# Reordering the last tiles' tails at the two hand-overs into the up projections of a two-layer decoder trunk

## The chip, the cores and the metric

One Trainium2 chip, one core of it. The metric is device time in microseconds (us) of the whole kernel, as the median of repeated runs; one further execution was profiled, and every duration below is from that one.

## The reference

An inference step of a two-layer trunk on 1024 prompt tokens and 64 sample tokens (8 x 8), width 1024, all in float32. Layer 0 is an S5 state-space mixer with a gated output, layer 1 a differential attention; each is followed by a convolutional feed-forward block. What matters here is the border between a mixer and its feed-forward block:

```python
out = gl[..., :D_MODEL] * jax.nn.sigmoid(gl[..., D_MODEL:])          # layer 0: gl = z @ glu_w
x = x + rmsnorm(a_out, p['a_post_g'][i])                             # layer 1: rmsnorm(o @ w_o, b_post_g)
f_out, buf = conv_ffn(rmsnorm(x, p['f_pre_g'][i]), ...)              # h = x @ w_up; conv over 3 tokens; gelu*val; @ w_down
```

Per token row there are so two norms between the mixer's matmul and the up projection `w_up` (1024 x 5632): one on the mixer's output, and, after the residual is added, one ahead of `w_up`.

## The kernel before

The 1088 tokens are nine row tiles: 0 to 7 are 128 prompt tokens each, the ninth (NTT) holds the 64 sample tokens. A float32 product is made of three matmuls on split operands (L815 to L817, `mm3`), a high part and a low part each; ScalarE (ACT) writes a high part (L150) and VectorE (DVE) the low part (L151).

**The mixer's end.** `glu` (layer 0) and `o_proj` (layer 1) go through the tiles in two batches, EARLY = sample, 0, 3, 1, 4 and LATE = 2, 5, 6, 7. For each finished tile they call `tail.add`, which does the following.

- `tail_a` (L847 to L861): loads the residual row tile into an `xr` slot by DMA (L853; there are two such slots), takes the sum of squares on ACT (L830), multiplies by the gain (L857), takes the reciprocal root (`rstd_from`), adds the residual (L860) and stores the row (L861).
- `tail.norm` for the tile before it: again a sum of squares and a reciprocal root, and the product with the gain (L870).
- `tail.pop`, once more than `lag` tiles are queued: the tile is transposed on TensorE (PE, L876) and split into `xT_hi` and `xT_lo` (`tail_b`). For tiles 3, 4 and 5 `Combos.pair` forms four differences with tile 0, 1 and 2 (L917 to L920), then five groups of four transposes; three of these go to the `Combos` tiles, which the up projection's seven-product scheme reads.

`lag` is 2 in `glu` and 1 in `o_proj`. With `root` off, `rstd_from` starts from an integer trick and makes three Newton steps of two small DVE instructions (L129, L136, L140); with it on, ACT takes a square root (L126), DVE a reciprocal (L127), and one step follows. `root` is off in `glu` and on from `ffn_down` on, so also in `o_proj`.

**The up projection.** `ffn_up` handles 22 inner tiles f. `inputs(f)` loads two 512 KB weight pieces, forms four sums in two `xr` slots (L1117 to L1120: `s12`, then `s34`), splits four operands on ACT and DVE and takes two `acc` slots, hg and hv. `first(f)` makes seven products of 12 matmuls each for the tiles 0 to 5; `rest(f, s)` then makes two products of 24 matmuls over tiles 6, 7 and the samples. For f = 0 the two are interleaved with the tails that are still open:

```python
        inputs(0)
        g = first(0)
        for _ in range(3):
            next(g)
            tail.pop()
```

The three parts of `first(0)` are: two products with tiles 0 to 2 (24 matmuls, with the copy L1154 of the first into hv between them); four products with the pair sums and tiles 3 to 5; one more with pair sums. So ahead of this loop the queue holds tiles 5, 6, 7 after `glu`, and 6, 7 after `o_proj`, all of them normed by a last `tail.norm()`.

**What sets the order.** The tile framework orders the instructions of each engine ahead of time by its own simulated timeline (`schedule_with_timeline_sim=True`): the order of the program gives the priority, readiness in that timeline decides. So the first weights of `inputs(0)` stand among the last tiles of `glu` in the trace. On the chip each engine takes its instructions in the order so fixed, and SP issues all the DMAs named here from one queue. Slots: `acc` has 14 buffers, of which 8 hold the Combos, one each the two gains (`post` and the gain of the second norm) and four the LATE rows; `gr` has 5, `xr` 2, `raw` (weights as loaded) 2. A new tile waits until its slot is given back.

Of the kernel before, what the change touches and what calls it, by code (L numbers as in the profile page):

```python
# [21 lines left out]
D = 1024  # L22
# [51 lines left out]
def trunk_kernel(ctx, tc, I, O):  # L74
# [30 lines left out]
    x1d = dpool.tile([T, D], F32, tag="x1d", name="x1d")  # L105
# [657 lines left out]
    EARLY, LATE = ORDER_O[:5], ORDER_O[5:]  # L763
# [40 lines left out]
    def slot(tag, shape=None, dtype=F32):  # L804

        al = {"gx": "acc", "post": "acc", "junk": "gr"}
        shp, bufs = {"acc": ([P, 2 + SEQ + NB * 10], NACC), "gx": ([P, 4, 2 * P], NACC), "gr": ([P, 512], NGR),
                     "xr": ([P, D], 2), "junk": ([P, D], NGR), "post": ([P, D], NACC),
                     "cvo": ([P, 4, 18], 2), "cpar": ([P, 2 * NF, 20], 1), "ss": ([P, 1], 4)}[tag]
        tag = al.get(tag, tag)  # L810
        return pools["ph"].tile(shape or shp, dtype, tag=tag, name=nm(tag), bufs=bufs)
# [7 lines left out]
    def tokens(tt):  # L819
        return (tt * P, P) if tt < NTT else (SEQ, TS)  # L820

    def row_bcast(src):
        t = slot("post")
        nc.sync.dma_start(t, src.partition_broadcast(P))
        return t

    def square_sum(y, n):
        junk = slot("junk", dtype=BF16)
        ss = slot("ss")
        A.activation(junk[0:n, 0 : y.shape[1]], y, AF.Square, accum_out=ss[0:n])  # L830
        return ss[0:n]
# [15 lines left out]
    def tail_a(y, tt, post, xsrc, xdst, last=False, rest=slice(0, D), aside=False, xr=None):  # L847


        t0, n = tokens(tt)  # L850
        if xr is None:
            xr = slot("xr")
            nc.sync.dma_start(xr[0:n], xsrc(tt))  # L853
        halves = (slice(512, D), slice(0, 512)) if last else (slice(0, D),)
        ss = square_sum(y[:, rest], n)
        for hs in halves if last else (rest,):
            V.tensor_tensor(y[:, hs], y[:, hs], post[0:n, hs], ALU.mult)  # L857
        r = rstd_from(pools["ph"], ss, 1, n, "n1", bufs=4, pre=sums.pop(tt, None), aside=aside, root=tail.root)
        for hs in halves:
            V.scalar_tensor_tensor(y[:, hs], y[:, hs], r[0:n], xr[0:n, hs], op0=ALU.mult, op1=ALU.add)  # L860
            nc.sync.dma_start(xdst(tt)[:, hs], y[:, hs])  # L861
# [17 lines left out]
    def tail_b(y, tt, scale=None):  # L879

        t0, n = tokens(tt)
        for h in range(2):
            split_evac(xh[:, 4 * h : 4 * h + 4, t0 : t0 + n], xl[:, 4 * h : 4 * h + 4, t0 : t0 + n],
                       transposed(y[:, 512 * h : 512 * h + 512], n), scale)
# [6 lines left out]
    class Combos:  # L891
        def __init__(self):
            self.tiles = [slot("acc", [P, 3, HT], F32R) for _ in range(8)]
# [32 lines left out]
    class Tail:  # L926
# [3 lines left out]
        def __init__(self):  # L930
            self.n, self.q, self.combos, self.gain, self.lag = [], [], None, None, 2

            self.root = False

        def add(self, y, tt, *a, aside=False, **kw):
            tail_a(y, tt, *a, aside=aside, **kw)
            self.norm()
            self.n.append((y, tt, aside))
            if len(self.q) > self.lag:
                self.pop()  # L940

        def norm(self):
            for a in self.n:
                tail_n(*a, self.gain)
            self.q += [a[:2] for a in self.n]
            self.n = []
# [10 lines left out]
    tail = Tail()  # L957
# [9 lines left out]
    def x_scr(buf):  # L967
        def f(tt):
            t0, n = tokens(tt)
            return buf[t0 : t0 + n]  # L970
        return f
# [31 lines left out]
    def fold_sample(dst, ps, t=None):  # L1003

        t = slot("gr") if t is None else t
        A.copy(t[0:TS], ps[TS : 2 * TS])
        V.tensor_tensor(dst, ps[0:TS], t[0:TS], ALU.add)
# [15 lines left out]
    def glu(ws):  # L1023

        zt = slot("acc")[0:TS, 0:D]
        zv = zt.rearrange("r (b g c) -> r b g c", g=8, c=16)
        for u in range(3):
            for j in range(min(3, 8 - 3 * u)):
                zs = zsd.rearrange("(b u) r w -> u r b w", u=3)[u, 32 * j : 32 * j + NB]
                nc.sync.dma_start(zv[:, :, 3 * u + j], zs.rearrange("s b (t c) -> (s t) b c", c=16))  # L1030
        post = row_bcast(I["a_post_g"][0])
        tail.gain = row_bcast(I["f_pre_g"][0])
        ao = {}


        for q, tts, end in ((0, ORDER_U, ()), (1, ORDER_U, ()), (2, EARLY, ()), (3, ORDER_O, EARLY), (2, LATE, LATE)):
            if q or end:
                ws = glu_units(q)
            qs_ = slice(q * 256, (q + 1) * 256)
            for tt in tts:  # L1040
                t0, n = tokens(tt)
                if tt in EARLY and q == 0 or tt in LATE and end is LATE:
                    ao[tt] = slot("acc")
                if end is LATE:
                    for cs in (slice(0, 512), slice(768, D)):
                        nc.sync.dma_start(ao[tt][:, cs], aod[t0 : t0 + n, cs])
                if q == 0 and tt == ORDER_U[4]:
                    tail_b(zt, NTT)
                    xsx = sample_pair()
                ps = tok_mm(tt, ws, None if n == P else xsx)  # L1050
                if n < P:
                    g = slot("gr")[0:n]
                    fold_sample(g, ps)
                else:
                    g = ps
                sg = slot("gr")[0:n]
                A.activation(sg[:, 0:256], g[:, 256:512], AF.Sigmoid)
                yq = ao[tt][0:n, qs_] if tt in ao else sg[:, 256:512]
                V.tensor_tensor(yq, g[:, 0:256], sg[:, 0:256], ALU.mult)
                if tt in end:  # L1060
                    if tt == 0:
                        tail.combos = Combos()
                    tail.add(ao[tt][0:n, 0:D], tt, post, x_in, x_scr(x1d), rest=qs_, aside=tt in EARLY)
                else:
                    part(yq, tt, post, qs_)
                    if tt in LATE:
                        nc.sync.dma_start(aod[t0 : t0 + n, qs_], yq)
                        tail.norm()
                        tail.pop()
            if q == 0:  # L1070
                conv_params(0)
                lam_column(cpool)
        tail.norm()


    NPAR = 20
# [20 lines left out]

    def ffn_up(i, down):
        cp = pools["cpar"]
        tail.gain = None  # L1100
        wv = I["w_up"][i].rearrange("(kt p) f -> p kt f", p=P)
        u3 = lambda t: t.rearrange("p (k f) -> p k f", f=P)

# [123 lines left out]

        inputs(0)
        g = first(0)
        for _ in range(3):  # L1230
            next(g)
            tail.pop()
        while tail.q:
            tail.pop()
        for s in range(2):
# [770 lines left out]
    def o_proj():  # L2006

        ws = half_units(I["w_o"][0], 1)
        post = row_bcast(I["b_post_g"][0])
        tail.gain, tail.lag, tail.root = row_bcast(I["f_pre_g"][1]), 1, True  # L2010
        conv_params(1)
        xsx = sample_pair()

        for half, tts in ((1, ORDER_O), (0, LATE)):
            if half == 0:
                ws = half_units(I["w_o"][0], 0)
            hs = slice(512 * half, 512 * half + 512)
            os_ = slice(512 - 512 * half, D - 512 * half)
            for tt in tts:
                if tt == 0 and half:  # L2020
                    tail.combos = Combos()
                t0, n = tokens(tt)
                end = half == 0 or tt in EARLY
                if end:
                    y = slot("acc")[0:n, 0:D]
                    nc.sync.dma_start(y[:, os_], yod[t0 : t0 + n])
                    if half:
                        part(y[:, os_], tt, post, os_)
                    yh = y[:, hs]
                else:  # L2030
                    yh = slot("gr")[0:n]
                ps = tok_mm(tt, ws, xsx)
                if n == P:
                    A.copy(yh, ps)
                else:
                    fold_sample(yh, ps)
                if end:
                    tail.add(y, tt, post, x_scr(x2d), x_scr(x3d), rest=hs, aside=tt in EARLY)
                else:
                    part(yh, tt, post, hs)  # L2040
                    nc.sync.dma_start(yod[t0 : t0 + n], yh)
                    tail.norm()
                    tail.pop()
        tail.norm()

    dtile = lambda name, shape: dpool.tile(shape, F32, tag=name, name=name)
    x2d = dtile("x2d", [T, D])
    gd = dtile("gd", [NF, P, TG])
    aod = dtile("aod", [SEQ, D])
    x3d = dtile("x3d", [T, D])  # L2050
# [62 lines left out]
```

## Time and profile before

| | |
|---|---|
| median of 3 runs | 2666.85 us (2663.87 to 2669.19) |
| the profiled execution | 2665.99 us, its span 2664.1 us |
| PE matmul busy | 2493.7 us, 94% |
| DVE busy | 1947.8 us, 73% |
| ACT busy | 1281.0 us, 48% |
| POOL busy | 661.2 us, 25% |
| chain that ended last | PE 58%, DVE 13%, DMA 4%, issue 4%, ACT 3%, POOL 3% |

Busy time is time in which an engine executes; the chain that ended last is followed back from the last instruction, at each step to what released it. The share of busy time is a mean over stages: the two stretches that the change touches, some 36 us each, are read by themselves. They are called hand-over 1 (after `glu`, 434.8 to 471.4 us) and hand-over 2 (after `o_proj`, 1888.9 to 1924.6 us).

### The profile page before, as it was taken

Reading aid. Unit: us, or ns where it says so; the run is one execution under the profiler, and the core shown is the slowest. Engines: PE = TensorE matmul, PEld = TensorE weight load, DVE = VectorE, ACT = ScalarE, POOL = GpSimd, SP = SyncE. Lnnn points to the kernel's source line nnn. Section 1 sums busy time; section 2 is a strip of 40 time slices with the busy share of each in tenths; the row PEclk is TensorE's granted clock in tenths of the full one; section 3 lists DMA queues with packets and bytes.
Section 4 is the critical chain, followed back from the end, with each engine's and each line's share of the span. In section 5 each row is a group of like instructions: output and inputs, shape, how many; then the busy total and the mean of one; then the engine's idle time right before and its main releaser. Section 6 shows DMA issues by size and latency. Waiting matters only on the chain.

```text
span 2664.1 us, 39516 instructions
## 1 busy us (share of the span) xinstructions
PE 2493.7 (94%) x14234; PEld 2199.5 (83%) x14234; DVE 1947.8 (73%) x3543; ACT 1281.0 (48%) x2597; POOL 661.2 (25%) x1062
## 2 busy tenths in 40 slices
PE   3778998999999999999999899999899999998997
PEld 2777876999999977788777788877799999996776
DVE  7994358677777789984222688875877777778999
ACT  6763234444444454354322677764544444444433
POOL 3220030111111176501201222113011111127571
PEclk9999998999999999999999899999899999999999
DMA  5443233122222233445646333325322222233334
GB/s 144 104 97 88 84 126 126 58 76 78 85 72 78 81 117 97 125 134 183 207 158 210 104 83 96 98 93 173 127 69 79 75 75 74 75 98 105 92 107 154
DMA packets 265688, 286.77 MB, mean 108 GB/s; under 512 B 42268, under 2 KB 212564, under 8 KB 265492
## 3 DMA queue, kind: packets, MB, share of 16 engines
q1 hardware_dynamic: 261892, 273.55, 33.3%
q0 software_dynamic: 3088, 9.77, 1.7%
q8 instruction: 113, 1.85, 0.3%
q10 hardware_dynamic: 512, 0.92, 0.1%
q14 instruction: 83, 0.68, 0.1%
HBM read 193.58 MB, written 70.93 MB: 99 GB/s over the span
## 4 chain that ended last, share of the span: by engine, by line
PE 58%; DVE 13%; DMA 4%; issue 4%; ACT 3%; POOL 3%; SPq 0%; DVEq 0%; ACTq 0%; POOLq 0%
PE mm L815 17%; PE mm L817 17%; PE mm L816 17%; DVE acc L1437 2%; PE mm L1426 2%; DVE xT_lo L151 2%; DMA gr<-gd 2%; DVE S L1907 1%; ACT S L1911 1%; DVE xT_hi L151 1%; DVE wst L151 1%; PE mm L1935 1%; PE tr L876 1%; DVE acc L860 1%; POOL xr L1306 1%
## 5 line engine op out<-in xcount | busy, mean ns | idle before, releaser
L815 PE MATMUL mm<-xT_hi,whi 128*128 128x384 f32 (+1 forms) x1408 | 457.0, 325 | 2.0 <-ACT acc L1154 1.7
L816 PE MATMUL mm<-xT_lo,whi 128*128 128x384 f32 (+1 forms) x1408 | 456.2, 324 | 1.4 <-DVE xT_lo L151 1.4
L817 PE MATMUL mm<-xT_hi,wlo 128*128 128x384 f32 (+1 forms) x1408 | 454.0, 324 | 0.0
L815 PEld LDWEIGHTS mm<-xT_hi,whi 128*128 128x128 f32 x1408 | 265.4, 189 | 3.8 <-ACT acc L1154 2.4
L816 PEld LDWEIGHTS mm<-xT_lo,whi 128*128 128x128 f32 x1408 | 265.7, 189 | 2.2 <-DVE xT_lo L151 2.1
L817 PEld LDWEIGHTS mm<-xT_hi,wlo 128*128 128x128 f32 x1408 | 265.3, 189 | 0.8
L1203 POOL COPY cvo<-acc 128x2 f32<-128x2 f32 x88 | 54.2, 616 | 814.1 <-ACT acc L1186 814.0
L815 PE MATMUL mm<-whi,xT_hi 128*128 128x512 f32 x608 | 242.9, 404 | 5.8 <-ACT whi L798 5.8
L1200 DVE SCALAR_TENSOR_TENSOR acc<-acc,cpar,acc 128x1104 f32<-128x1104 f32 x176 | 239.9, 1385 | 4.7 <-ACT acc L1198 4.7
L816 PE MATMUL mm<-wlo,xT_hi 128*128 128x512 f32 x608 | 242.8, 400 | 0.1
L817 PE MATMUL mm<-whi,xT_lo 128*128 128x512 f32 x608 | 242.2, 400 | 0.0
L150 ACT CAST whi<-raw 128x1024 fp32r<-128x1024 f32 x88 | 92.7, 1053 | 248.5 <-PE mm L817 245.1
L1437 DVE TENSOR_TENSOR acc<-mm,acc 128x512 f32<-128x512 f32 x279 | 184.3, 679 | 8.4 <-PE mm L817 8.1
L151 DVE TENSOR_TENSOR wlo<-raw,whi 128x1024 fp32r<-128x1024 f32 x88 | 107.7, 1224 | 103.5 <-PE mm L816 90.8
L815 PE MATMUL mm<-acc,whi 128*128 128x384 f32 x528 | 178.8, 339 | 2.5 <-DVE acc L1160 2.5
L817 PE MATMUL mm<-acc,wlo 128*128 128x384 f32 x528 | 178.9, 339 | 0.0
L816 PE MATMUL mm<-acc,whi 128*128 128x384 f32 x528 | 178.3, 338 | 0.0
L815 PEld LDWEIGHTS mm<-whi,xT_hi 128*128 128x128 f32 x608 | 115.3, 190 | 36.9 <-ACT whi L798 6.2
L816 PEld LDWEIGHTS mm<-wlo,xT_hi 128*128 128x128 f32 x608 | 115.2, 189 | 27.9 <-DVE wlo L799 0.8
L817 PEld LDWEIGHTS mm<-whi,xT_lo 128*128 128x128 f32 x608 | 114.9, 189 | 27.9 <-issue 0.8
L1198 ACT ACTIVATE acc<-acc,cpar 128x1104 f32<-128x1104 f32 x88 | 114.2, 1313 | 18.1 <-DVE acc L1169 11.9
L1186 ACT COPY acc<-mm 128x256 f32<-128x256 f32 x88 | 32.4, 369 | 183.7 <-PE mm L817 183.7
(575 smaller groups left out, 6311.6 us busy)
## 6 DMA issues: line engine op xcount, KB each, us to landing
raw<-in_w_up_dram SPq DMA_DIRECT2D x88, 512.0 KB
gd<-acc SPq DMA_DIRECT2D x44, 552.0 KB
raw<-in_w_down_dram SPq DMA_DIRECT2D x44, 512.0 KB
gr<-gd SPq DMA_DIRECT2D x80, 256.0 KB
raw<-in_glu_w_dram SPq DMA_DIRECT2D x40, 256.0 KB
acc<-in_cache_k_dram SPq DMA_DIRECT2D x16, 512.0 KB
acc<-in_cache_v_dram SPq DMA_DIRECT2D x16, 512.0 KB
xj<-in_x_prompt_dram SPq DMA_DIRECT2D x8, 512.0 KB
```

What stands on the lines that cost most here:

```text
L150: A.copy(hi_ap, ps_ap)
L151: V.tensor_tensor(lo_ap, ps_ap, hi_ap.bitcast(F32), ALU.subtract)
L815: PE.matmul(out, lh, rh, start=start, stop=False, **kw)
L816: PE.matmul(out, lh, rl, start=False, stop=False, **kw)
L817: PE.matmul(out, ll, rh, start=False, stop=stop, **kw)
L860: V.scalar_tensor_tensor(y[:, hs], y[:, hs], r[0:n], xr[0:n, hs], op0=ALU.mult, op1=ALU.add)
L1186: A.copy(hb[:, 2 + n0 : 2 + SEQ], ps[:, 0:wp])
L1198: A.activation(hc, hb[:, 2 : 2 + TG], AF.Identity, bias=cp[:, ft, 3:4], scale=cp[:, ft, 2:3])
L1200: V.scalar_tensor_tensor(hc, hb[:, tap : tap + TG], cp[:, ft, tap : tap + 1], hc, op0=ALU.mult, op1=ALU.add)
L1203: GP.tensor_copy(co[:, 0:2], hb[:, SEQ : SEQ + 2])
L1426: PE.matmul(pa[h], lt, wt[:, h * 512 : (h + 1) * 512], start=st and j == 0, stop=sp and j == len(seq) - 1)
L1437: V.tensor_tensor(a, ps, a, ALU.add)
```

## The change

- `Tail.last` takes the place of `add` for tile 7, the last of LATE: it pops the tile that is queued (5, a pair) at once and only notes tile 7's arguments.
- `Tail.end` does tile 7's `tail_a`, sets `root` on ahead of it, norms tile 6 and lists tile 7 for its norm. `ffn_up` calls it after the first part of `first(0)`, calls `tail.norm()` for tile 7 after the second, and pops both after the third.
- `lag` is 1 for LATE in `glu` too, and is put back to 2 at `glu`'s end; the last `tail.norm()` of `glu` and `o_proj` is gone.

```diff
+        def last(self, *a, **kw):
+            self.pop()
+            self.late = a, kw
+
+        def end(self):
+            (y, tt, *a), kw = self.late
+            self.root = True
+            tail_a(y, tt, *a, **kw)
+            self.norm()
+            self.n.append((y, tt, False))
...
                 if end is LATE:
+                    tail.lag = 1
...
-                    tail.add(ao[tt][0:n, 0:D], tt, post, x_in, x_scr(x1d), rest=qs_, aside=tt in EARLY)
+                    put = tail.last if tt == LATE[-1] else tail.add
+                    put(ao[tt][0:n, 0:D], tt, post, x_in, x_scr(x1d), rest=qs_, aside=tt in EARLY)
...
-        tail.norm()
+        tail.lag = 2
...
     def ffn_up(i, down):
         cp = pools["cpar"]
-        tail.gain = None
...
-        for _ in range(3):
-            next(g)
-            tail.pop()
+        next(g)
+        tail.end()
+        next(g)
+        tail.norm()
+        next(g)
+        tail.gain = None
         while tail.q:
             tail.pop()
...
-                    tail.add(y, tt, post, x_scr(x2d), x_scr(x3d), rest=hs, aside=tt in EARLY)
+                    put = tail.last if tt == LATE[-1] else tail.add
+                    put(y, tt, post, x_scr(x2d), x_scr(x3d), rest=hs, aside=tt in EARLY)
...
-        tail.norm()
```

## Rows read from the trace of the kernel before

**Rows 1.** Page, busy us (share of the span) and instructions of each engine.

```profile
PE 2493.7 (94%) x14234; PEld 2199.5 (83%) x14234; DVE 1947.8 (73%) x3543; ACT 1281.0 (48%) x2597; POOL 661.2 (25%) x1062
```

**Rows 2.** Windows, hand-over 1: us; busy PE, PEld, DVE, ACT, POOL; PEclk (granted); DMA.

```profile
440.00:445.00 5.00, 0.00 (x0) 0.00 (x0) 4.96 (x21) 1.33 (x3) 0.00 (x0) 0.75 0.23 94
450.00:455.00 5.00, 3.87 (x15) 3.47 (x14) 5.00 (x9) 2.77 (x5) 0.31 (x2) 0.50 0.50 150
...
sum 36.40, PE 24.99 PEld 23.58 DVE 30.07 ACT 15.18 POOL 1.46; mean PE 3.57 PEld 3.37 DVE 4.30 ACT 2.17 POOL 0.21
```

**Rows 3.** The windows of hand-over 2, their sum.

```profile
sum 35.60, PE 25.48 PEld 23.78 DVE 32.45 ACT 18.37 POOL 2.25; mean PE 3.64 PEld 3.40 DVE 4.64 ACT 2.62 POOL 0.32
```

**Rows 4.** Timeline of PE in hand-over 1: start, us, engine, line [idle before <-releaser].

```profile
448.76 1.09 PE L876 MATMUL tr<-ident,gr 128*128 128x128 f32 x4 [9.75 <-DVE gr L917]
...
457.23 0.34 PE L816 MATMUL mm<-xT_lo,whi 128*128 128x384 f32 x1
457.40 0.34 PE L817 MATMUL mm<-xT_hi,wlo 128*128 128x384 f32 x1
...
459.14 0.60 PE L876 MATMUL tr<-ident,gr 128*128 128x128 f32 x4
459.49 0.42 PE L816 MATMUL mm<-acc,whi 128*128 128x384 f32 x1
...
471.38 0.31 PE L816 MATMUL mm<-xT_lo,whi 128*128 128x320 f32 x1
```

**Rows 5.** Timeline of DVE in hand-over 1.

```profile
437.77 1.28 DVE L860 SCALAR_TENSOR_TENSOR acc<-acc,rr,xr 128x1024 f32<-128x1024 f32 x1
438.97 1.28 DVE L870 SCALAR_TENSOR_TENSOR acc<-acc,rr,acc 128x1024 f32<-128x1024 f32 x1
...
440.23 0.68 DVE L1117 TENSOR_TENSOR xr<-raw 128x512 f32<-128x512 f32 x1
...
442.75 1.23 DVE L151 TENSOR_TENSOR wlo<-xr,whi 128x1024 fp32r<-128x1024 f32 x1
...
444.33 1.28 DVE L860 SCALAR_TENSOR_TENSOR acc<-acc,rr,xr 128x1024 f32<-128x1024 f32 x1
...
446.73 0.68 DVE L1119 TENSOR_TENSOR xr<-raw,raw 128x512 f32<-128x512 f32 x1
...
447.93 0.68 DVE L917 TENSOR_TENSOR gr<-acc,acc 128x512 f32<-128x512 f32 x1
...
460.47 1.28 DVE L870 SCALAR_TENSOR_TENSOR acc<-acc,rr,acc 128x1024 f32<-128x1024 f32 x1
```

**Rows 6.** Timeline of POOL and ACT in hand-over 1: hv's slot and the copy into it.

```profile
450.77 0.10 POOL L1129 MEMSET acc<- 128x2 f32 x1 [11.66 <-PE tr L876]
...
452.16 0.47 ACT L1154 COPY acc<-mm 128x384 f32<-128x384 f32 x1
```

**Rows 7.** Waits of PE in hand-over 2: line <- what released it, us, times, longest.

```profile
PE tr L876 <- DVE acc L870: 5.9, 1, 5.9
PE mm L815 <- DVE acc L1160: 2.5, 1, 2.5
PE mm L816 <- DVE xT_lo L151: 1.1, 1, 1.1
```

**Rows 8.** Timelines of DVE and PE in hand-over 2.

```profile
1898.27 0.68 DVE L917 TENSOR_TENSOR gr<-acc,acc 128x512 f32<-128x512 f32 x1
...
1924.60 0.31 PE L815 MATMUL mm<-xT_hi,whi 128*128 128x320 f32 x1
```

**Rows 9.** DVE lines in hand-over 1: xcount, busy us, mean ns, idle before.

```profile
L136 DVE SCALAR_TENSOR_TENSOR rs<-rr,rv 128x1 f32<-128x1 f32 x13 | 2.4, 214 | 0.0
```

**Rows 10.** ACT lines, whole run: loads of the table that holds the square root.

```profile
L126 ACT ACT_TABLE_LOAD x3 | 3.8, 1283 | 0.1
```

**Rows 11.** SP's queue in hand-over 1 (residual of tile 7), and one residual load on the chain.

```profile
430.31 0.42 SPq L853 DMA_DIRECT2D xr<-in_x_prompt_dram  x1
...
1827.37 3.75 DMA xr<-x2d
```

More of the change, by code (lines that the diff above doesn't have):

```diff
@@ L933, in __init__ @@
             self.root = False
+            self.late = None
         def add(self, y, tt, *a, aside=False, **kw):
```

## The prediction

> **What bounds the kernel now.** The page comes first: PE is busy 94% of the span and DVE 73% [rows 1], so a reordering can only win where PE stands still or runs at half its clock. The reader then goes to the two stretches in which the mixer's last tiles run out and the up projection begins. In hand-over 1 PE does nothing for a whole window, then works at a granted clock of 0.50, which is 1.2 of its 2.4 GHz, while DVE is busy 4.96 and 5.00 of 5 us [rows 2].
>
> What is lost there follows from the work. The seven products of `first(0)` are 84 matmuls, 0.173 us apart at full clock (457.23 to 457.40), which is 14.5 us. Tiles 2, 5, 6 and 7 need 44 transposes, four of which take 0.35 us (459.14 to 459.49), so 3.9 us. Together 18.4 us [rows 4]. In hand-over 1 the first matmul of `rest` starts at 471.38, and one product of f = 1 (12 x 0.173 = 2.1 us) has already slipped in ahead of it: of the 36.4 us, 36.4 - 2.1 - 18.4 = 15.9 us are lost. In hand-over 2 `rest` starts at 1924.60 [rows 8]; of the 35.6 us, 17.2 are lost. The pool is 33 us.
>
> The waits then say to whom it goes. In hand-over 1 it is one wait of 9.75 us, for the pair's first difference L917 [rows 4]. Tile 5 was normed by 438.97 + 1.2 = 440.2, but L917 started only at 447.93: DVE first did the first weight sums (L1117), a low part (1.23 us), tile 7's residual sum (444.33), tile 6's norm and the third weight sum (446.73) [rows 5]. hv is another victim: its slot came free with the pair's transposes (450.77), and the copy L1154, behind which the second product waits, ran at 452.16 [rows 6]. In hand-over 2 the longest wait, 5.9 us, is for tile 2's norm (L870), then come 2.5 us for L1160, which stood in DVE's queue, and 1.1 us for a low part [rows 7]. There the pair began at 1898.27 already [rows 8], because `lag` was 1.
>
> **The change, part by part, against the profiled execution of 2665.99 us.** DVE is full in both stretches, so I first bound what any order could give, by DVE's work that must be done ahead of `rest`.
>
> Hand-over 1: DVE's 30.07 us [rows 2] contain the four sums of `inputs(1)` (4 x 0.68 = 2.7, by the duration at 446.73) and one low part of its weights (1.23) [rows 5]; both can wait. With `root` on for three roots, two of three Newton steps fall away in each, 12 small instructions of about 2.4/13 = 0.18 us [rows 9], 2.2 us (L140 taken as its partner L136; the reciprocal replaces L129). With `lag` 1, tile 2's two low parts (2 x 0.68 = 1.4) move in among tile 7's matmuls. What is left is 30.07 - 2.7 - 1.2 - 2.2 - 1.4 = 22.6 us: `rest` at 457.6 at the earliest, against 471.4 - 2.1 = 469.3 now, a gain of 11.7 at most.
>
> Hand-over 2: `root` and `lag` already stand, so only 2.7 + 1.2 come off 32.45 [rows 3]; 1889 + 28.5 = 1917.5 against 1924.6, a gain of 7.1 at most.
>
> **The pair at once.** In hand-over 1 L917 can follow tile 5's norm at 440.2 in place of 447.93, 7.7 us earlier; PE's 9.75 us shrink to about 2, and hv's slot comes as much earlier. One weight sum (0.68) may still come ahead. I take 7.0. The lower end: the residual of tile 7, now behind `s12` in the two `xr` slots, lands late and the whole load stands on the path, 0.42 + 3.75 [rows 11], so -4.2; the upper end is 11.7. In hand-over 2 the pair is early anyway; what can go is the queue before L1160, 2.5 us [rows 7], and I take that; tile 2's wait isn't touched. Lower end: `s12` gets the slot that tile 7's residual had, so two sums and a low part (0.68 + 0.68 + 1.23 = 2.6) can get ahead of tile 2's norm, -2.6; upper end 7.1.
>
> **Tile 7's tail and two norms behind the weights.** Moved are, per hand-over, the residual load of 512 KB (SP; issued at 430.31 now [rows 11]), the sum of squares, the product with the gain, the root, the residual sum, the store of the row, and for tiles 6 and 7 a sum of squares, a root and a product of 1.28 us. Nothing is added to DVE. I cost the move at nothing on PE as long as first(0)'s 14.5 us of products hide it. If the cover is short, `rest` waits: from the end of `s12`'s low part, issue and load (4.2) and the sum and norm (2 x 1.28 with ACT's work between) must pass. On SP the load stands behind the weight loads of `inputs(0)`, long issued, and at worst behind those of `inputs(1)`; queued behind it are the row stores and later weights, for which nobody waits in these 20 us.
>
> **The root on ACT in hand-over 1.** One more table load of 1283 ns [rows 10] and three short activations. ACT is busy 15.18 of 36.4 us [rows 2], so I take 0, with ends 0 and -1.3. The Trainium skill, ScalarE: Activation LUTs, section on table sets, speaks against this: calls should be batched by set, and it prices a switch at about 2.7 us in that section; by that figure on the path the sum would be 2659.2 in place of 2656.5. The trace's load of 1283 ns is half of it, and no row shows one inside a hand-over with PE waiting on it alone.
>
> The `lag` set back and the gain's None moved cost nothing: no instruction.
>
> **Sum.** 7.0 + 2.5 = 9.5 us: 2665.99 - 9.5 = 2656.5 for this execution. It lay 0.9 below the median of 2666.85, so 2657.4 for the median. Ends: a gain of 11.7 + 7.1 = 18.8 (2648.1) and a loss of 4.2 + 2.6 + 1.3 = 8.1 (2675).
>
> **The rivals.**
> *The wait only moves (20%).* The work on DVE stays, and what PE no longer waits for at the pair it waits for at `rest`, on tile 7's norm, which ended at 461.7 while PE had products to run [rows 5]. For it: DVE at 5.00 of 5. Against: PE then has f = 1's first product to take, as now. A gain of 0 to 5: 2662 to 2667.
>
> *The order stays (7%).* The planner places by readiness in its own timeline; where it holds the weight sums ready earlier than tile 5, the trace keeps its order. Against: the pair now has the higher priority. 2666 to 2668.
>
> *Slower: tile 7's residual at the head of DVE's queue (14%).* The load waits for `s12`'s slot; if the planner puts L860 of tile 7 ahead of the low parts of `s34` or the pair, these stand behind a DMA. Price per hand-over: 4.2, one weight load ahead of it in SP's queue (another 3.75 [rows 11]), and PE back at half clock: at 0.50 the 3.87 us of PE in one window [rows 2] lose half, 1.9. That is 9.9, twice 19.7, less the 9.5: 2677 for the median. It decides from a stall of 9.5/2 = 4.8 us in each. Against: the slot is free from `s12`'s low part, which the new order brings forward. The Trainium skill, TensorE: Matmul & The Clock Gate, in its passage on engine queue depths, calls DVE's queue strictly first in, first out; by that this rival has its force, and the trace agrees: L917 stood 7.7 us behind others though its inputs were there.
>
> **How the numbers follow.** 59% for the forecast (2648 to 2661.5), 20, 7 and 14 for the rivals. A measurement can tell 0.2%, 5.3 us, from no change, so faster is below 2661.5: the forecast and a touch of the first rival, 0.60. Same takes the rest of that rival, the second, and nothing else, 0.26; slower 0.14. The range 2648 to 2670 holds the first three cases and leaves out the slower one beyond it.
>
> **What would show it.** Right: L917 of hand-over 1 within 2 us of tile 5's L870, PE's wait there near 2 us, `rest` of f = 0 some 25 us (not 34) after glu's last matmul net of f = 1's product; L1160 in hand-over 2 without a wait. Wrong: a wait of PE for tile 7's low part or transposes of over 4 us, an L860 released by a DMA, L917 still behind L1119, or a first product cut off from its second by hv's slot.

## The result, and the profile after

The changed kernel takes 2671.12 us (median of 20 runs, 2667.82 to 2676.25), the kernel before 2666.03 us (20 runs beside them, 2662.15 to 2669.68). The ratio is 1.0022, with a 95% interval of 1.0016 to 1.0028: slower by 4.3 to 7.5 us, where 9.5 us less had been forecast. The span of the profiled execution is 2668.7 us. The page's first part answers to [rows 1]:

```profile
PE 2493.2 (93%) x14234; PEld 2200.6 (82%) x14234; DVE 1952.4 (73%) x3531; ACT 1279.9 (48%) x2601; POOL 617.6 (23%) x1062
```

The work is the same, and DVE has 12 instructions less, as forecast for the root. From L931 on the lines of the changed kernel are up to 17 higher: L1126 loads a weight piece, L1131 to L1134 form the weight sums, L1168 is the copy into hv.

**Hand-over 1.** The windows that answer to [rows 2]; the third covers the whole stretch, with its sums in it:

```profile
440.00:445.00 5.00, 2.25 (x11) 2.28 (x12) 3.81 (x5) 1.11 (x2) 0.24 (x2) 0.77 0.99 292
450.00:455.00 5.00, 5.00 (x24) 4.96 (x23) 4.87 (x14) 3.50 (x10) 0.00 (x0) 0.71 0.15 61
...
434.80:471.20 36.40, 27.95 (x157) 26.81 (x158) 28.69 (x62) 15.64 (x32) 0.55 (x5) 0.91 0.31 98
```

PE no longer stands for a whole window, and is busy 27.95 us where it was 24.99. Its timeline tells what became of the wait of 9.75 us [rows 4]:

```profile
435.64 0.44 PE L816 MATMUL mm<-xT_lo,whi 128*128 128x384 f32 x1 [0.90 <-DVE xT_lo L151]
442.75 1.09 PE L876 MATMUL tr<-ident,gr 128*128 128x128 f32 x4 [4.92 <-DVE gr L917]
...
448.20 0.66 PE L876 MATMUL tr<-ident,gr 128*128 128x128 f32 x4 [2.65 <-DVE xT_lo L151]
...
467.12 0.31 PE L816 MATMUL mm<-xT_lo,whi 128*128 128x320 f32 x1
```

The wait for the pair is 4.92 us, and two waits for low parts, of 2.65 and 0.90 us, stand beside it. DVE's timeline, which answers to [rows 5], shows why:

```profile
437.06 1.29 DVE L860 SCALAR_TENSOR_TENSOR acc<-acc,rr,xr 128x1024 f32<-128x1024 f32 x1
438.38 0.69 DVE L1133 TENSOR_TENSOR xr<-raw,raw 128x512 f32<-128x512 f32 x1
438.99 0.68 DVE L1134 TENSOR_TENSOR xr<-raw,xr 128x512 f32<-128x512 f32 x1
439.59 1.28 DVE L870 SCALAR_TENSOR_TENSOR acc<-acc,rr,acc 128x1024 f32<-128x1024 f32 x1
440.78 1.23 DVE L151 TENSOR_TENSOR wlo<-xr,whi 128x1024 fp32r<-128x1024 f32 x1
441.93 0.68 DVE L917 TENSOR_TENSOR gr<-acc,acc 128x512 f32<-128x512 f32 x1
...
445.72 1.23 DVE L151 TENSOR_TENSOR wlo<-raw,whi 128x1024 fp32r<-128x1024 f32 x1 [1.90 <-ACT whi L150]
446.86 0.69 DVE L920 TENSOR_TENSOR gr<-acc,gr 128x512 f32<-128x512 f32 x1
447.46 0.68 DVE L151 TENSOR_TENSOR xT_lo<-tr,xT_hi 128x512 fp32r<-128x512 f32 x1
```

The last two weight sums (438.38, 438.99) now go ahead of tile 5's norm, and a low part between that norm and L917, which starts at 441.93. With all four sums made this early the two `raw` buffers come free, and the next inner tile's first weight gets into the middle of the pair: at 445.72 DVE stands 1.90 us for its high part. ACT in turn had waited for that weight's DMA, which SP issued at 439.14:

```profile
444.64 1.05 ACT L150 CAST whi<-raw 128x1024 fp32r<-128x1024 f32 x1 [3.89 <-DMA raw<-in_w_up_dram]
```

L920 and tile 5's low part, which PE wants, stand behind that weight in DVE's order. The Trainium skill, TensorE: Matmul & The Clock Gate, in its passage on engine queue depths, calls DVE's queue strictly first in, first out; the trace agrees, 1.90 us of standing with L920 and the low part behind it.

**Hand-over 2.** The waits of PE from 1880 to 1926 us (line, what released it, us, times, longest), which answer to [rows 7]:

```profile
PE tr L876 <- DVE acc L870: 8.1, 2, 6.7
PE tr L876 <- DVE gr L917: 2.2, 1, 2.2
PE mm L816 <- DVE xT_lo L151: 1.7, 1, 1.7
PE tr L876 <- DVE xT_lo L151: 1.2, 1, 1.2
```

The wait of 2.5 us for L1160 is gone. The 8.1 us for L870 are two waits in PE's timeline:

```profile
1897.13 1.94 PE L876 MATMUL tr<-ident,acc 128*128 128x128 f32 x8 [6.74 <-DVE acc L870]
...
1921.36 0.63 PE L876 MATMUL tr<-ident,acc 128*128 128x128 f32 x4 [1.33 <-DVE acc L870]
```

The first is for tile 2's norm and grew from 5.9 to 6.7 us; the second is for the norm of tile 7, which the change put late and for which PE did not wait before. There are also waits for L917 and for a low part of the pair. DVE started tile 5's norm at 1903.03 and L917 at 1906.53, where it had been 1898.27 [rows 8], behind the last two weight sums (1899.31, 1899.90) and low parts:

```profile
1898.10 1.22 DVE L151 TENSOR_TENSOR wlo<-xr,whi 128x1024 fp32r<-128x1024 f32 x1
...
1901.89 1.22 DVE L151 TENSOR_TENSOR wlo<-xr,whi 128x1024 fp32r<-128x1024 f32 x1
1903.03 1.28 DVE L870 SCALAR_TENSOR_TENSOR acc<-acc,rr,acc 128x1024 f32<-128x1024 f32 x1
1905.39 1.23 DVE L151 TENSOR_TENSOR wlo<-raw,whi 128x1024 fp32r<-128x1024 f32 x1 [1.08 <-ACT whi L150]
1906.53 0.69 DVE L917 TENSOR_TENSOR gr<-acc,acc 128x512 f32<-128x512 f32 x1
```

**Where the time went.** Both kernels run the same 14,234 matmuls and transposes. So the traces can be laid side by side: the start of the matmul with the same number ends a stage, at places where the two orders agree again. A step is the time of a stage less its time in one further execution of the kernel before (span 2665.8 us, the first experiment). In the change three stages move. "Last head" is the end of the attention, 1768 to 1813 us, where its last head runs out into the output projection; the change does not touch it.

| kernel, us | hand-over 1 | up projection, layer 0 | last head | hand-over 2 | ratio (95%) |
|---|---|---|---|---|---|
| before, first profile | -0.9 | 0.0 | 0.0 | 0.0 | 1 |
| the change | -3.4 | 0.0 | **+3.9** | **+2.5** | 1.0022 (1.0016 to 1.0028) |
| hand-over 1 only | -4.0 | 0.0 | +3.7 | 0.0 | 1.0003 (0.9994 to 1.0011) |
| hand-over 2 only | -2.1 | 0.0 | +0.8 | 0.0 | 1.0007 (0.9998 to 1.0016) |
| residual early | -4.4 | +0.1 | -1.1 | -0.3 | 0.9986 (0.9977 to 0.9995) |
| pair at once alone | -1.9 | +4.8 | +1.0 | +0.3 | 1.0048 (1.0035 to 1.0062) |
| residual early, hand-over 1 only | -3.6 | +0.1 | -0.1 | -0.1 | 0.9987 (0.9978 to 0.9996) |
| without root | -0.8 | +4.9 | -1.1 | 0.0 | 1.0032 (1.0021 to 1.0043) |
| lag alone | -0.9 | +7.7 | +3.9 | -0.6 | 1.0057 (1.0044 to 1.0069) |
| change, old order of last head | -5.3 | 0.0 | +0.1 | -0.1 | 1.0000 (0.9991 to 1.0009) |
| hand-over 1, old order of last head | -4.4 | 0.0 | +0.2 | -1.1 | 1.0001 (0.9991 to 1.0010) |
| before, new order of last head | -2.7 | 0.0 | +3.9 | +0.4 | 1.0025 (1.0014 to 1.0036) |

How far one execution can be trusted is seen at hand-over 1: four executions with the old source there gave 0 (the one compared with), -0.9, -2.1 and -2.7, while PE's granted clock over the 38 us from 434 was 0.78 in the first of them and 0.87 in the last. These four mean -1.4, the six with the change there (two of them with the residual early) -4.2. So in the profiled executions hand-over 1 gained 2.8 us; PE's waits say nearly the same: 9.7 + 1.1 + 0.3 + 0.2 = 11.3 us before, 4.9 + 2.7 + 0.9 + 0.2 = 8.7 after. A profiled execution can lie up to 5 us from its kernel's median (4.9 above it with `lag` alone, 5.1 below it with hand-over 1 and the old order), so the ratios are firmer than sums of steps.

### The profile page after: what moved, and what is told of

It reads as the page before. It is cut to its first block, busy times and chain, and to the rows that moved or that the text cites. A ratio compares the mean times of both kernels' runs of the same rounds, so it can differ in the third digit from the quotient of the medians.

```text
span 2668.7 us, 39527 instructions
## 1 busy us (share of the span) xinstructions
PE 2493.2 (93%) x14234; PEld 2200.6 (82%) x14234; DVE 1952.4 (73%) x3531; ACT 1279.9 (48%) x2601; POOL 617.6 (23%) x1062
## 5 line engine op out<-in xcount | busy, mean ns | idle before, releaser
L1217 POOL COPY cvo<-acc 128x2 f32<-128x2 f32 x88 | 48.0, 546 | 839.4 <-ACT acc L1200 839.3
L1924 DVE CUSTOM_DVE_ANT_0 S<-mm,tb 128x512 f32<-128x512 f32 (+3 forms) x192 | 101.4, 552 | 22.9 <-PE mm L1922 19.5
```

The costliest lines, as they stand in the source:

```text
L1217: GP.tensor_copy(co[:, 0:2], hb[:, SEQ : SEQ + 2])
L1924: V.tensor_tensor_reduce(S_[j][:, k0 : k0 + w], ps[:, 0:w], H["tb"][:, b0 : b0 + w], 0.125, -3e38, ALU.add, ALU.max, mx[:, j, c : c + 1])
```

## The experiments

**The kernel before once more**, for the scale of the comparison.

> The kernel before, once more, for the spread of a stage from one execution to the next. If stages are steady: every landmark (start of hand-over 1, of the attention's last head, of hand-over 2) within 1 us of the first profile once the start is aligned; theory C wants 3 us and more between the same landmarks.

Measured 2667.61 us in its one run, the span 2665.8. Against it the first profile differs by +2.4 us at 1236 to 1340 us and by -3.3 us at 1723 to 1745, stages that no kernel here edits; steps are read only where several executions agree.

**One hand-over alone.** `last` and the new loop are used where `tail.late` was set, the old path where it was not. First hand-over 1 only, with these lines of `o_proj` put back:

```diff
-                    put = tail.last if tt == LATE[-1] else tail.add
+                    put = tail.add
...
+        tail.norm()
```

> The change at hand-over 1 alone; o_proj and hand-over 2 as before. Theory A (three places: hand-over 1 gains, hand-over 2 loses, and the shift of the planner's timeline reorders the last head of the attention): hand-over 1 gains 2 to 3 us, the stretch 1765 to 1800 loses 4 to 5, hand-over 2 is as before; together 0 to 4 us slower. Theory B (all of the loss sits in hand-over 2): 2 to 4 us faster. Theory C (what differs between the traces outside the hand-overs is chance of one execution): 2 to 4 us faster too, with the attention's stretch as before.

Ratio 1.0003 (0.9994 to 1.0011). The gain at hand-over 1 is there (-4.0), and 3.7 us are lost again 1300 us later, at the last head, in a stage with the same source text.

Then hand-over 2 only, the same lines of `glu` put back and its `tail.lag = 1` gone:

> The change at hand-over 2 alone; glu and hand-over 1 as before. Theory A: 2 to 4 us slower, all of it in hand-over 2, where the pair's first difference starts some 6 us later than before; the attention's order as before. Theory B: 5 us slower, the whole of the measured loss. If the postponed tail is harmless there: within 1 us.

Ratio 1.0007 (0.9998 to 1.0016); the step at hand-over 2 is 0.0, neither the forecast's gain nor the 2.5 us that the whole change lost there. PE's waits in the same window:

```profile
PE tr L876 <- DVE acc L870: 8.4, 2, 7.4
PE mm L816 <- DVE xT_lo L151: 1.7, 1, 1.7
PE mm L815 <- ACT acc L1167: 1.5, 1, 1.5
```

The wait for L1160 is gone here too. In its place tile 2's norm is waited for longer (7.4 us in place of 5.9), tile 7's norm for 1.1, and the copy into hv (L1167 here) for 1.5, where it was 0.6.

**Tile 7's residual loaded early**, in `last`, so that it holds its `xr` slot while the first inner tile's weights are made, as it did before:

```diff
         def last(self, *a, **kw):
             self.pop()
-            self.late = a, kw
+            t0, n = tokens(a[1])
+            xr = slot("xr")
+            nc.sync.dma_start(xr[0:n], a[3](a[1]))
+            self.late = a, dict(kw, xr=xr)
```

> The change, but tile 7's residual is loaded where it was before, in the call that notes the tile, so that it takes the slot that it had. Slot theory (the postponed load hands its slot to the weight sums of the first inner tile, these free the raw buffers early, and the weights of two inner tiles get ahead of tile 5's norm and of the pair): in hand-over 2 the pair starts again within 2 us of where it was before, in hand-over 1 it follows tile 5's norm; 3 to 7 us faster than before. Rival (the postponed tail itself comes late at the rest product): no better than the change, 3 to 5 us slower than before.

Ratio 0.9986 (0.9977 to 0.9995): one DMA issued earlier makes the change faster than the kernel before. L917 started at 437.75 and 1894.14, and the last head's order was again that of before. By the steps, most of the difference from the change lies in the last head (5.0 us) and hand-over 2 (2.8), and only 1.0 in hand-over 1. Two things changed at once, the slot and the planner's order, so the next runs part them.

**The pair at once, without the move of tile 7's tail** (`lag` 1 in LATE, `root` off):

```diff
         def last(self, *a, **kw):
             self.pop()
-            self.late = a, kw
+            self.add(*a, **kw)
+            self.norm()
```

> The pair at once and lag 1 in glu, but tile 7's tail and both norms straight behind it, ahead of the first inner tile's weights; root as before. Slot theory: tile 7's residual keeps its slot, so hand-over 1 gains as much as with the residual loaded early, 3 to 5 us, and hand-over 2 nothing (within 1 us). The planner's order of the attention's last head differs from before's here too, another order than the change's: if a changed order there costs in itself, plus 1 to 5 us in that stage; if only the change's own order is bad, 0. If postponing the tail is what gains: hand-over 1 within 1 us of before.

Ratio 1.0048 (1.0035 to 1.0062), an outright loss, in neither hand-over: 4.8 us in layer 0's up projection, and 4.6 more in the stage from 1032 to 1235 us. The expected gain of 3 to 5 us at hand-over 1 did not come either: -1.9 lies among the 0 to -2.7 of the old source, although L917 started at 436.52 and PE waited only 2.2 us for it.

**Residual early, hand-over 1 only:**

> The change with tile 7's residual loaded early, at hand-over 1 alone; everything from the attention on is planned as before. If the steps of the stages add: hand-over 1 gains 3 to 4.5 us, all other stages within 1 us of before, together 0.11 to 0.17% faster. If the gain of the third experiment came from hand-over 2 or the attention: same as before.

Ratio 0.9987 (0.9978 to 0.9996). Past hand-over 1 PE's order is that of before but for four instructions, and its distance from the kernel before is the same at 2402 us as behind hand-over 1, within 0.3 us. PE's longest waits from 425 to 475 us:

```profile
PE mm L815 <- DVE acc L1180: 2.9, 1, 2.9
PE tr L876 <- DVE gr L917: 2.2, 1, 2.2
```

and, in SP's timeline, the load of the next inner tile's first weight:

```profile
449.79 0.38 SPq L1129 DMA_DIRECT2D raw<-in_w_up_dram  x1
```

With its slot held, that load moves from 439.14 to 449.79, behind the pair, and L917's wait comes down to 2.2 us, close to the forecast's 2. Yet PE's waits still sum to 8.9 us, against 8.7 with the change itself: they moved to a product's sum (L1180). So the slot sets which wait it is, and hardly how much.

**Without `root`**, the change less one line:

```diff
-            self.root = True
```

> The change, but the three roots of hand-over 1 by Newton steps as before. By my term for root (12 small DVE instructions, 2.2 us of DVE's time ahead of the rest product): hand-over 1 gains 1 to 2 us less than the change's 2.5 to 3.4. If DVE isn't what bounds it: within 0.7 us of the change. The attention's last head is planned in another order than with root: if the change's order there is the price, that stage costs less than 3.9 us here.

Ratio 1.0032 (1.0021 to 1.0043), 0.0010 above the change with intervals that overlap, though the last head fell to -1.1: layer 0's up projection lost 4.9 us and the stage from 1032 us 4.5. At hand-over 1 the step is -0.8, so nothing of the gain is left where a gain smaller by 1 to 2 us was expected. PE waits 1.2 us there for a Newton step (L140), which it does not in the change; as the order behind it differs too, how much of this is the root's own is open.

**`lag` 1 alone**, in the kernel before:

```diff
                 if end is LATE:
+                    tail.lag = 1
...
         tail.norm()
+        tail.lag = 2
```

> The kernel before with lag 1 for LATE in glu and nothing else. If the early transposes and the pair ahead of the weights are the whole gain of hand-over 1: 2 to 4 us there. If the pair must also come ahead of tile 7's tail: under 1.5 us. The attention's last head is planned in another order than before: 0 to 4 us lost in that stage, nothing in hand-over 2.

Ratio 1.0057 (1.0044 to 1.0069); 7.7 us in layer 0's up projection, 6.6 behind it, 3.9 at the last head. Hand-over 1, the only place that the line concerns, kept its time (-0.9). The windows of 490 to 935 us, in the kernel before run again, then with `lag` alone:

```profile
490.00:935.00 445.00, 445.00 (x2719) 443.23 (x2719) 322.75 (x363) 192.21 (x275) 51.66 (x162) 1.00 0.24 77
```

```profile
490.00:935.00 445.00, 441.16 (x2676) 434.58 (x2675) 313.50 (x356) 193.94 (x271) 106.87 (x160) 1.00 0.23 75
```

With the order that `lag` alone gets, PE has gaps in a stretch that it filled before, 43 matmuls fewer fit in, and POOL's busy time doubles with about as many instructions. PE's waits in this stretch are 2.4 us (two) for POOL's copy L1206 and 1.2 us (six) for DVE, where the kernel before has none; POOL's copies of line L1205 take 1922 ns each where the same 40 (L1203 there) take 525 ns in the kernel before. Why they take longer was not followed further. In this kernel, the one without `root` and the pair alone, PE's order differs from that of before through the whole of layer 0's up projection; in the change it differs only at hand-over 1 there.

**The last head's order held fixed.** In the programs, PE's order in the change differs from that of before in four places: hand-over 1, the last head, hand-over 2 and layer 1's up projection. The last three experiments fix 575 PE instructions around the last head in a given order, by order-only dependencies, and leave the planner free in the rest. A helper records PE's instructions, so PE's lines are L100 or L101 there, and the others are 39 or 40 higher than in the kernel that it starts from.

```diff
-    PE = nc.tensor
+    PE = Pinned(nc.tensor, [r + j for r, n in PIN_ORDER for j in range(n)])
...
+                    for x, y in zip(self.want, self.want[1:]):
+                        tc.add_manual_dep(self.got[y], self.got[x].name,
```

First the whole change with the old order:

> The whole change, with TensorE's 575 instructions around the attention's last head (about 1760 to 1815 us, some 1300 us behind the first edit) held in the order that they have in the kernel before; nothing else is touched, and PE's order there is then that of before. Theory A (the planner's new order of the last head costs 3.9 us, hand-over 1 gains 3 to 4 us, hand-over 2 loses 2.5 us): the step of the last head falls from +3.9 us to within 1 us of before, and the ratio to between 0.9985 and 1.0010; with hand-over 2 still +2.5 us, the ratio stands near 1.000. Theory B (the whole loss is made at hand-over 2, and the last head's 3.9 us come of what runs there, not of its order): the last head's step stays at 3 to 4 us and the ratio at 1.0022. Theory C (the steps are one execution's chance): no step keeps its size, ratio 1.0022 within its interval.

Ratio 1.0000 (0.9991 to 1.0009), the last head's step +0.1. Hand-over 2, with the change still in it, came to -0.1, so its loss of 2.5 us was the planner's order too, and this ratio has both put right: L917 started at 1894.50 there, and the waits were

```profile
PE tr L100 <- DVE acc L909: 8.3, 2, 7.4
PE mm L100 <- DVE xT_lo L190: 1.7, 1, 1.7
PE mm L100 <- ACT acc L1207: 1.1, 1, 1.1
```

as with hand-over 2 alone. What the order does at the last head is seen in PE's timeline, in the change first:

```profile
1781.82 0.40 PE L817 MATMUL mm<-qx,xT_lo 128*128 128x512 f32 x1
...
1782.28 1.04 PE L876 MATMUL tr<-ident,kr 128*128 128x128 f32 x8
1783.15 0.27 PE L1946 MATMUL tr<-ident,S 128*128 128x128 f32 x1
1785.01 0.49 PE L1952 MATMUL mm<-v,wt 128*128 128x128 f32 x2 [1.58 <-ACT wt L1947]
...
1787.18 0.74 PE L876 MATMUL tr<-ident,kr 128*128 128x128 f32 x4 [0.92 <-DVE rs L136]
1787.58 0.77 PE L815 MATMUL mm<-qwh,xT_hi 128*128 128x512 f32 x1
```

and in the change with the old order:

```profile
1777.40 1.04 PE L100 MATMUL tr<-ident,kr 128*128 128x128 f32 x8
1778.19 0.72 PE L100 MATMUL mm<-kl,xT_hi 128*128 128x512 f32 x2
...
1781.07 0.27 PE L100 MATMUL tr<-ident,S 128*128 128x128 f32 x1
...
1782.08 0.49 PE L100 MATMUL mm<-v,wt 128*128 128x128 f32 x2
1782.40 0.60 PE L100 MATMUL tr<-ident,kr 128*128 128x128 f32 x4
1782.76 0.48 PE L100 MATMUL mm<-qwh,xT_hi 128*128 128x512 f32 x1
```

In the old order twelve projection matmuls stand behind the eight transposes of kr and cover ACT's work on wt. In the new one such matmuls run ahead of these transposes and none is left behind them: PE stands 1.58 and 0.92 us, and the matmuls behind run at about half clock: 0.77 us for the first where the old order has 0.48, at a granted clock of 0.76 and 0.67 in the two windows of 3 us from 1786. With one more wait, of 1.16 us at 1799.63 where the old order has 0.78, the waits make 2.9 us; the clock of the two windows, (0.24 + 0.33) x 3, is an estimated 1.7 us more.

That is more than the 3.9 us of the table, and so is the stage up to this point: from 1775 to 1802 us the four executions with the change's order lost 5.1 to 5.5 us, seven with the old order 0.0. Some 1.5 us of it come back right behind, because in the execution compared with PE's clock fell there and not in the change (first the kernel before run again, then the change):

```profile
1805.00:1820.00 15.00, 15.00 (x78) 11.86 (x76) 5.50 (x9) 4.57 (x6) 0.00 (x0) 0.89 0.73 230
```

```profile
1805.00:1820.00 15.00, 14.84 (x73) 11.30 (x73) 6.36 (x9) 4.83 (x7) 0.00 (x0) 1.00 0.81 247
```

The old order does not always bring that fall: four of its eight executions have it, and none of the four with the change's order. So the new order costs some 3.9 to 5.4 us, by which execution it is compared with.

Then hand-over 1 alone with the old order:

> Hand-over 1 of the change alone, with TensorE's instructions of the attention's last head held in the order of the kernel before. Theory A: the 4.0 us that hand-over 1 gained in the profile of that part alone are no longer given back at the last head (3.7 us there): ratio 0.9980 to 0.9992, faster than before by 2 to 4 us. Theory B (the order of the last head is of no account): ratio 1.000 as hand-over 1 alone had, and a step of 3 to 4 us at the last head.

Ratio 1.0001 (0.9991 to 1.0010). The step fell from 3.7 to 0.2 as expected, but the expected ratio of 0.9980 to 0.9992 was missed; the 2.8 us of the table alone would be 0.9990, just outside the interval; but PE's order in layer 1's up projection is not that of before here either (a step of +0.6). The profiled execution was the fastest of this kernel's 11 runs, so its steps are no measure of the median. With the residual early, in the run on hand-over 1 alone, the times gave 0.9987, a gain of 1 to 6 us with the same order elsewhere. What hand-over 1 is worth by itself without that load stays open, between nothing and some 2.5 us.

Last, the kernel before with the change's order at the last head:

> The kernel before, with no part of the change, but with TensorE's 575 instructions around the attention's last head held in the order that the changed kernel gives them. Theory A: slower than before by the step at the last head alone, 3 to 4 us, ratio 1.0010 to 1.0018; nothing moves at hand-over 1. Theory B: no difference, ratio within 0.0008 of 1, and no step at the last head over 1 us.

Ratio 1.0025 (1.0014 to 1.0036), above the 1.0010 to 1.0018 expected, of which its interval covers a part; the step is +3.9, with the same wait as in the change:

```profile
1785.66 0.49 PE L101 MATMUL mm<-v,wt 128*128 128x128 f32 x2 [1.59 <-ACT wt L1970]
```

The granted clock fell in the same window of 15 us too, to 0.94 (0.92 in the change):

```profile
1775.00:1790.00 15.00, 12.25 (x63) 9.68 (x62) 5.78 (x24) 6.38 (x18) 0.00 (x0) 0.94 0.50 169
```

With no line of the change in it, the kernel before becomes as slow as the changed one. Its order in layer 1's up projection is the change's as well, but the step there is +1.1 us, no more than the +1.3 of the change with the old order of the last head.

## Why the prediction was wrong

**The sum had two stages, and the time was set in a third.** The steps from the table, -2.8 (the mean) + 3.9 + 2.5 and 0.8 in layer 1's up projection, give +4.4 us against the measured +4.3 to +7.5; with the 5.3 us lost from 1775 to 1802 in place of 3.9 it would be +5.8. That stage stands in no line of the prediction: it took the order outside the two hand-overs as given. The rival that the order stays considered the planner, but only at the place of the edit. The run with the new order alone and the one with the old order restored (which set hand-over 2 right with it) show the cause from both sides. That the planner's own timeline shifted there because hand-over 1 ended earlier in it is argued, not shown; why the order in between stayed is open.

**The pair at once, forecast 7.0: mis-sized.** Hand-over 1 gained 2.8 us in the profiles and by the times between nothing and some 2.5. L917 did come earlier, but the wait shrank by 4.8 us, not 7.7. The step that failed is that only one weight sum of 0.68 us would come ahead. Two sums and a low part did, and then the next inner tile's weight inside the pair cost 2.65 us more. The prediction had the cause in its own lower bound, the slot that tile 7's residual gives up, but applied it to hand-over 2 alone. Nor is the 2.8 the pair's own: with the pair as early but `root` off, with or without the postponed tail, hand-over 1 showed no gain (-0.8 and -1.9). The rival in which the wait only moves, with a gain of 0 to 5, had the size of this stage, but not the place: PE waited inside the pair, not at `rest` for tile 7's norm.

**Hand-over 2, forecast 2.5: the term failed.** The wait for L1160 went, as said. But tile 2's norm, whose wait the prediction did not touch, was waited for 0.8 us longer (1.5 with hand-over 2 alone), and the move of tile 7's tail, put at nothing because the products would hide it, cost a wait of 1.3 us for tile 7's norm (1.1 alone). By itself hand-over 2 is worth 0.0. With the planner's order in the whole change it is -2.5, and that this is near the -2.6 of the prediction's lower end is in part luck: two weight sums do stand ahead of tile 2's norm, as there, but the greater part is the pair's, with waits of 2.2 and 1.2 us for L917 and a low part.

**The root, forecast 0 on the path: right for its work.** One more table load of 1283 ns ran in hand-over 1, from 448.87, and no wait of PE there was for it. By the Trainium skill, ScalarE: Activation LUTs, section on table sets, a switch costs about 2.7 us; the trace has 1.30, ACT's next work starting at 450.17. The run without the root was not faster. The prediction put the saved Newton steps at nothing on the path too, and there it may have been too low: with the Newton steps left in, hand-over 1 showed no gain, and the planner's order cost 4.9 and 4.5 us in two later stages.

**The slower rival** had the sign and not the place: in hand-over 1 tile 7's residual sum ran at 452.16 with DVE not idle ahead of it, so no load stood at the head of the queue, and 2671.12 is not its 2677. The 14% given to slower, with all of it in one local mishap, were too few because no case covered a reordering elsewhere.

## What to carry to other kernels

Where a planner orders the whole program by its own timeline, a local edit can change the order far away: compare each engine's order of the two programs first, and price every stretch that differs, not the edit alone. A stretch found so can be pinned, as here, which parts the worth of an edit from the luck of the order; one line of `lag` moved this kernel by 0.57% without changing the stage it stands in. A moved step also gives up its buffer, and what takes that buffer can go ahead of the work that was to be hurried: with tile 7's residual loaded early, PE's wait for the pair fell from 4.9 to 2.2 us. That version is the fastest here (0.9986, and 0.9987 for hand-over 1 alone, against 1.0022), but by the steps most of that comes of the order that the planner then gave the last head and hand-over 2.

## What was not expected of the hardware

Two short waits of PE, 1.58 and 0.92 us within 4 us with only 128-wide transposes and matmuls between them, were followed by matmuls at half clock (0.77 and 0.63 us, back to 0.40 us by 1791.11; granted 0.51 from 1787.5 to 1790.5). With the projection matmuls in between, as the old order has them, PE ran at a granted clock of 1.00 from 1775 to 1790:

```profile
1775.00:1790.00 15.00, 15.00 (x80) 12.17 (x79) 7.69 (x24) 6.80 (x20) 0.00 (x0) 1.00 0.47 159
```

So the waits of an order can cost more than their own length: an estimated 1.7 us of clock here on top of 2.9. What decides it the waits alone do not show. The same wait of 2.14 us was followed by half clock in the kernel before run again (at 1803.33, matmuls of 0.63 us) and by full clock in the change (at 1805.16, 0.40). So the clock also differs between executions of one order: 0.78 to 0.87 over hand-over 1, in executions whose times there differ by 2.7 us, as much as the change's whole gain.
